# The order of the gate, up and down block products of a SwiGLU on one Trainium2 core: one by one in a mixed order, or in runs

## The chip, the cores and the metric

The kernel runs on one core of a Trainium2 chip. A core has TensorE (matmuls, results in PSUM, a memory of eight banks), VectorE, ScalarE, GpSimd (POOL in the rows) and SyncE (SP in the rows), which here issues all transfers. Each engine works through its own queue in order; engines wait for each other by semaphores. The metric is the device time of one execution in microseconds (us), the median of several.

## The reference

One encoder layer on 768 tokens (512 and 256) of width 1024, in fp32. A token mixer with three kinds of heads comes first, then

```
def swiglu(x, w_gate, w_up, w_down):
    return (jax.nn.silu(x @ w_gate) * (x @ w_up)) @ w_down

x = layer_norm(DEEPNORM_ALPHA * x + mix, ...)
x = layer_norm(DEEPNORM_ALPHA * x + swiglu(x, w_gate, w_up, w_down), ...)
```

The hidden width is 2816, that is 22 blocks of 128, worked on as 11 pairs of blocks. The change concerns the SwiGLU alone.

## The kernel before

Every fp32 operand of a matmul is split into a high and a low part (`split`, L112: a cast on ScalarE, L113, and a subtraction on VectorE or GpSimd, L114), and a product is three matmuls: high by high, high by low, low by high.

For a pair of hidden blocks, x @ w_gate, x @ w_up and the product with w_down are each a 2 by 2 block product, done with seven block products in place of eight. The seven have the names 1, 2, 6, 5, 7, 3, 4 and run in this order (`PRODUCTS`); g1 is product 1 of the gate, u4 product 4 of the up, d6 product 6 of the down part. A gate or up product is 12 matmuls of 384 columns (`gate_up`, L997, matmul L1010), a down product 9 of 512 (`down`, L1034, matmul L1043).

The sums that link the seven lie in PSUM. In the gate and up part, products 1, 6, 7 and 4 add up in one bank (bank 0 for g and u alike), 5 and 3 in another, 2 in bank 1. Between them results are taken out: after 1, 6 and 5 ScalarE copies the bank ("snap", L1021), after 2, 7 and 3 VectorE adds bank and snap (L1026), then silu (L933, gate) or the multiply with the silu (L936, up). Product 4 is read straight out of its bank, by silu or by the multiply that is called the drain below. In the down part products 1, 6, 7, 4 add up in three banks (one for each of three groups of tokens) and 2, 5, 3 in three others; after each product VectorE adds the bank into y (L1048), three adds of 512 columns.

Seven hidden blocks feed the down products: `gated` (L935) makes them after the up products, with four sums on GpSimd (L945 to L949), and splits them into seven places of `mix`, the last three in `gated_rest`.

Pair p's gate and up products run together with the down products of pair p - 1, for p = 1 to 9 (L1102 to L1111). Pair 0 stands before (`first_pair`), pair 10 and the last two down parts after. TensorE's order is the program's. The other engines' order is made by a scheduler at build time.

Weights come in blocks of 512 KB (tile `raw`, L121) into three buffers, in the order of `raws` in `_ff_items` (L1126): two of g, two of d, two of u. A block's buffer is free when its last split or sum is done. GpSimd makes the sums of blocks that products 6, 5 and 7 need (L168; L180 for the down part, after product 5's split). The split operands lie in five tiles `w` of two operands each, in the order of `items`. `op_done` (L211) frees a tile when the product with its second operand is done, and `pump` then issues up to two more splits (none after a down product).

Of the kernel before, what the change touches and what calls it, by code (L numbers as in the profile page):

```python
# [27 lines left out]
NP = NFF // 2  # L28
NP_ST = 9
PRODUCTS = (1, 2, 6, 5, 7, 3, 4)  # L30
OUT_ORDER = [6, 7, 2, 3, 4, 0, 1, 5]


# [25 lines left out]
def encoder_layer(ctx: ExitStack, tc, a, o):  # L59
# [27 lines left out]
    def catch_up(until):  # L87
        saved = clock["now"]
        while queue and queue[0][0] <= until:
            at, _, f = heapq.heappop(queue)  # L90
            clock["now"] = at
            f()
        clock["now"] = saved

    def run(main):
        for cost, f in main:
            catch_up(clock["now"])
            f()
            clock["now"] += cost
# [4 lines left out]
    items, raw_order = _ff_items()  # L104
    raw_of = {key: W_FF + i for i, key in enumerate(raw_order)}
    n_raw, n_items = W_FF + len(raw_order), W_FF + len(items)
    w_tiles = {}
    w_state = {"dma": 0, "item": 0, "free": 3}
    w_raw, w_sum, raw_done = {}, {}, set()
    w2 = []  # L110

# [81 lines left out]
    def pump(most=99):  # L193
        while w_state["item"] < n_items:
            if w_ready(w_state["item"]):
                if most == 0:
                    break
                most -= 1
                w_split()
            elif w_state["dma"] < n_raw and (w_state["dma"] < 3 or w_state["dma"] - 3 in raw_done):  # L200
                w_load()
            else:
                break
# [6 lines left out]

    def op_done(key, prod):  # L211
        n = w_tiles.pop((key, prod))[1]
        if n % 2 == 1 or n == len(items) - 1:
            w_state["free"] += 1
        if w_state.get("after") is None:
            pump()
        else:
            with tc.issue_after(w_state["after"]):
                pump(AHEAD[key[0]])
# [7 lines left out]
    def load_x(k):  # L227
        raw = rawp.tile([P, 1024], F32, tag="raw", name="raw")
        if k > 0:
            nc.sync.dma_start(out=raw[:, :T], in_=a["xT"][k])  # L230
        return raw
# [34 lines left out]
    raws = {0: load_x(0)}  # L266
# [535 lines left out]
    def x1_block(name, m, k):  # L802
        if name in ("t3", "t4"):
            return mix[k + (4 if name == "t3" else 0)][:, m, :H2]
        return xb[name][:, m, k]
# [32 lines left out]
    def wout_mm(ps, t, half, i, first, last):  # L838
        w = w_tiles[W_OUT + 4 * half + i // 2]
        sl = slice((i % 2) * 512, (i % 2 + 1) * 512)  # L840
        for m, wi in ((0, 0), (0, 1), (1, 0)):
            TE.matmul(ps, lhsT=mix[OUT_ORDER[i]][:, m, t * P:(t + 1) * P], rhs=w[:, wi, sl],  # L842
                      start=(i == first and m == 0 and wi == 0), stop=(i == last and m == 1))
# [71 lines left out]
    def bank(i):  # L915
        if i < 4:
            return pff.tile([P, 512], F32, tag=f"p{i}", name="ff")
        return ps_one({4: "sc", 5: "sc", 6: "tp", 7: "av"}[i])
# [7 lines left out]
    def gt_block(i, m):  # L926
        return mix[i][:, m, H2:]
# [7 lines left out]
    def gated(i, src, p):  # L935
        V.tensor_tensor(out=HB[i], in0=src, in1=TH[i], op=ALU.mult)  # L936
        if p >= NP_ST:
            gt_split(4 * (p - NP_ST) + i, HB[i])
            return

        if i in (0, 2):
            gt_split(i // 2, HB[i])
        have.add(i)
        if i > 0 and {0, 1, 3} <= have and i != 2:
            G.tensor_tensor(out=S1, in0=HB[1], in1=HB[3], op=ALU.add)  # L945
            G.tensor_tensor(out=HB[1], in0=HB[0], in1=HB[1], op=ALU.subtract)
            G.tensor_tensor(out=HB[0], in0=S1, in1=HB[0], op=ALU.subtract)
        if len(have) == 4:
            G.tensor_tensor(out=HB[2], in0=HB[2], in1=HB[0], op=ALU.subtract)  # L949
            gt_split(2, HB[0])  # L950
            gt_split(3, S1)
            have.clear()
# [3 lines left out]
    def gated_rest():  # L956
        gt_split(4, HB[1])
        gt_split(5, HB[2])
        gt_split(6, HB[3])
# [37 lines left out]
    def gate_up(kind, p, banks):  # L997
        st = {}

        def step(prod, k):  # L1000
            if k == 0 and prod < 3:
                st[prod] = bank(banks[prod - 1])[:, :H2]
                if prod == 2:
                    st[5] = st[2]
            elif k == 0 and prod == 5 and len(banks) > 2:
                st[5] = bank(banks[2])[:, :H2]
            b = st[{2: 2, 5: 5, 3: 5}.get(prod, 1)]
            w = w_tiles[(kind, p), prod][0]
            for wi, m in ((0, 0), (0, 1), (1, 0)):
                TE.matmul(b, lhsT=w[:, wi, k * P:(k + 1) * P], rhs=x1_block(x_name[prod], m, k),  # L1010
                          start=(prod in (1, 2, 5) and k == 0 and wi == 0 and m == 0), stop=(k == 3 and wi == 1), skip_group_check=prod in (6, 7, 4, 3))
            if k == 3:
                after(prod)
                op_done((kind, p), prod)

        def after(prod):
            use = silu if kind == "g" else lambda i, src: gated(i, src, p)
            out = TH if kind == "g" else HB
            if prod in (1, 6, 5):
                st["s", prod] = t = wk2.tile([P, H2], F32, tag="snap", name="snap", bufs=2)  # L1020
                S.copy(out=t, in_=st[5 if prod == 5 else 1])  # L1021
            elif prod == 4:
                use(2, st[1])
            else:
                i, b, other = {2: (0, 2, 1), 7: (3, 1, 5), 3: (1, 5, 6)}[prod]
                w_state["after"] = V.tensor_tensor(out=out[i], in0=st[b], in1=st["s", other], op=ALU.add).ins  # L1026
                use(i, out[i])

        return lambda prods: [(0.48, lambda prod=prod, k=k: step(prod, k)) for prod in prods for k in range(4)]
# [4 lines left out]
    def down(p):  # L1034
        st = {}

        def step(prod, t):
            if prod < 3:
                st[prod, t] = bank(2 + t if prod == 1 else 5 + t)
            b = st[1 if prod in (1, 6, 7, 4) else 2, t]  # L1040
            w = w_tiles[("d", p), prod][0]
            for m, wi in ((0, 0), (0, 1), (1, 0)):
                TE.matmul(b, lhsT=gt_block(a_slot[prod], m)[:, t * P:(t + 1) * P], rhs=w[:, wi],  # L1043
                          start=(prod in (1, 2, 5) and m == 0 and wi == 0), stop=(m == 1),
                          skip_group_check=prod in (6, 7, 4, 3))
            for dt, c in {1: ((0, lo_half),), 2: ((0, lo_half),), 6: ((0, hi_half),), 5: ((3, hi_half),),
                          7: ((3, hi_half),), 3: ((0, hi_half),), 4: ((3, lo_half),)}[prod]:
                V.tensor_tensor(out=y[t + dt][:, c], in0=b, in1=y[t + dt][:, c], op=ALU.add)  # L1048
            if t == 2:
                op_done(("d", p), prod)  # L1050

        return lambda prods: [(0.64, lambda prod=prod, t=t: step(prod, t)) for prod in prods for t in range(3)]
# [49 lines left out]
    for p in range(1, NP):  # L1102
        g = gate_up("g", p, (0, 1, 7))
        if p <= NP_ST:
            u, d = gate_up("u", p, (0, 1)), down(p - 1)
            run(g(PRODUCTS))
            run(d(PRODUCTS[:4]))
            run(u(PRODUCTS))
            run(d(PRODUCTS[4:]))
            if p < NP_ST:  # L1110
                gated_rest()  # L1111
        else:
            u = gate_up("u", p, (2, 3))
            run(g(PRODUCTS))
            run(u(PRODUCTS))
    ln2 = load_ln(1)
# [9 lines left out]
def _ff_items():  # L1126

    items = [((kind, 0), prod) for kind in "gu" for prod in (11, 12, 21, 22)]
    raws = [((kind, 0), i) for kind in "gu" for i in range(2)]
    for p in range(1, NP):  # L1130
        items += [(("g", p), prod) for prod in PRODUCTS]
        raws += [(("g", p), i) for i in range(2)]
        if p <= NP_ST:
            items += [(("d", p - 1), prod) for prod in PRODUCTS[:4]]
            raws += [(("d", p - 1), i) for i in range(2)]
        items += [(("u", p), prod) for prod in PRODUCTS]
        raws += [(("u", p), i) for i in range(2)]
        if p <= NP_ST:
            items += [(("d", p - 1), prod) for prod in PRODUCTS[4:]]
    for p in range(NP_ST, NP):  # L1140
        items += [(("d", p), prod) for prod in (11, 12, 21, 22)]
        raws += [(("d", p), i) for i in range(2)]
    return items, raws


def _layout(inputs):
# [24 lines left out]
    subs += bv[0] + bqk[0] + au + bqk[1] + bqk[2] + bv[1] + av + bqk[3]  # L1171
    wo = np.concatenate([wout[k * P:(k + 1) * P] for k in OUT_ORDER], axis=0)
    for half in range(2):
# [59 lines left out]
```

## Time and profile before

| | us |
|---|---|
| median of 3 runs | 892.03 (890.7 to 892.97) |
| the profiled execution | 893.67 |
| its span, first to last instruction | 891.8 |
| nine pairs, g1 of pair 1 to g1 of pair 10 | 428.39 |
| VectorE busy in them | 376.59 |
| GpSimd busy in them | 239.91 |

Rows of a timeline give the start, the duration (several instructions of one kind merged into one row, with their count), the engine, the line, what is written from what, and in brackets how long the engine was idle before and what ended that. The duration of one instruction overlaps the next one's by some tens of ns, so the step from start to start is the cost in a full queue.

### The profile page before, as it was taken

To read this page: it belongs to the slowest core of one execution; us is meant where nothing else is said; L and a number is where in the kernel's file an instruction comes from. 1 tells how busy PE (TensorE), PEld (TensorE's weight loads), DVE (VectorE), ACT (ScalarE), POOL (GpSimd) and SP (SyncE) were. 2 spreads that over 40 slices of the span, in tenths; PEclk is the share of its full clock that TensorE was granted. 3 is DMA by queue.
4 is the path that set the end of the run, shared out by engine and by line. 5 is a ranking of instruction groups with operands and counts; after the bars stand their busy time and mean duration, and the time that the engine had idled before them with its cause. 6 is when DMAs were issued, how large, how long until landed. Compare 5 with 4: busy or idle time off the path is not lost. (4 is left out here: it accounts for less than half of the span.)

```text
span 891.8 us, 12955 instructions
## 1 busy us (share of the span) xinstructions
PE 846.5 (95%) x4811; PEld 754.3 (85%) x4811; DVE 666.9 (75%) x1168; ACT 422.0 (47%) x922; POOL 384.7 (43%) x320
## 2 busy tenths in 40 slices
PE   7999999999999998899999999999999999899996
PEld 6889897888987887898888898898888888789985
DVE  3574447576677568769989897988979797989577
ACT  3375477676665526544434444344444344344421
POOL 0580011100121148877655655555466464653235
PEclk9999999999999999999999999999999999999999
DMA  6830202011017101112212121222121222222222
GB/s 220 247 113 24 71 26 71 24 49 46 5 54 276 54 18 50 46 48 72 72 38 81 48 82 61 72 71 72 70 71 48 71 72 71 71 70 73 72 83 107
DMA packets 22160, 66.66 MB, mean 75 GB/s; under 512 B 3664, under 2 KB 5584, under 8 KB 22096
## 3 DMA queue, kind: packets, MB, share of 16 engines
q1 hardware_dynamic: 22096, 65.82, 22.4%
q8 instruction: 38, 0.62, 0.3%
q14 instruction: 26, 0.21, 0.1%
HBM read 62.67 MB, written 3.15 MB: 74 GB/s over the span
## 5 line engine op out<-in xcount | busy, mean ns | idle before, releaser
L114 DVE TENSOR_TENSOR w<-raw,w 128x512 fp32r<-128x512 f32 (+2 forms) x179 | 185.1, 1053 | 36.3 <-ACT w L113 35.4
L113 ACT CAST w<-raw 128x512 fp32r<-128x512 f32 (+2 forms) x213 | 138.3, 676 | 119.1 <-POOL raw L168 43.8
L1010 PE MATMUL ff<-x,w 128*128 128x384 f32 x600 | 109.9, 336 | 1.7 <-DVE bv L991 1.7
L1010 PEld LDWEIGHTS ff<-x,w 128*128 128x128 f32 x600 | 105.3, 188 | 3.5 <-DVE bv L991 2.0
L1010 PE MATMUL ff<-mix,w 128*128 128x384 f32 x480 | 91.8, 339 | 14.5 <-ACT snap L1021 6.5
L1010 PEld LDWEIGHTS ff<-mix,w 128*128 128x128 f32 x480 | 83.4, 188 | 19.3 <-DVE bv L1026 9.6
L444 PE MATMUL mm<-xhi,w 128*128 128x512 f32 x320 | 79.1, 346 | 0.4 <-DVE qs L341 0.4
L168 POOL TENSOR_TENSOR ws<-raw 128x512 f32<-128x512 f32 x29 | 41.2, 1424 | 79.2 <-DMA raw<-in_w 74.9
L168 POOL TENSOR_TENSOR raw<-raw 128x512 f32<-128x512 f32 x49 | 71.2, 1454 | 6.7 <-DVE w L114 3.5
L423 PE MATMUL mm<-w,xhi 128*128 128x256 f32 x384 | 71.4, 286 | 0.0
L842 PE MATMUL mm<-w,mix 128*128 128x512 f32 x270 | 68.3, 399 | 1.5 <-ACT tt L686 0.8
L1010 PE MATMUL ff<-xt,w 128*128 128x384 f32 x360 | 65.9, 335 | 0.0
L621 POOL TENSOR_TENSOR mn<-mn,neghalf 128x1 f32<-128x1 f32 x24 | 13.8, 574 | 116.6 <-DVE mn L620 112.8
L1010 PEld LDWEIGHTS ff<-xt,w 128*128 128x128 f32 x360 | 63.0, 188 | 0.0
L1043 PE MATMUL ff<-w,mix 128*128 128x512 f32 x216 | 58.2, 400 | 4.9 <-DVE y L1048 4.9
L842 PEld LDWEIGHTS mm<-w,mix 128*128 128x128 f32 x270 | 49.2, 188 | 12.6 <-ACT tt L686 1.3
L423 PEld LDWEIGHTS mm<-w,xhi 128*128 128x128 f32 x384 | 58.1, 189 | 1.4 <-issue 0.9
L444 PEld LDWEIGHTS mm<-xhi,w 128*128 128x128 f32 x320 | 49.1, 189 | 6.8 <-issue 0.8
L114 DVE TENSOR_TENSOR mix<-bv,mix 128x384 fp32r<-128x384 f32 x62 | 52.9, 856 | 2.1 <-ACT mix L113 2.0
L114 POOL TENSOR_TENSOR w<-raw,w 128x512 fp32r<-128x512 f32 x34 | 49.6, 1475 | 10.5 <-ACT w L113 10.2
L1043 PE MATMUL sc<-w,mix 128*128 128x512 f32 x189 | 50.4, 398 | 3.4 <-DVE y L1048 3.4
L423 PE MATMUL mm<-w,xlo 128*128 128x256 f32 x192 | 53.4, 278 | 0.0
(234 smaller groups left out, 1772.8 us busy)
## 6 DMA issues: line engine op xcount, KB each, us to landing
raw<-in_w SPq DMA_DIRECT2D x95, 512.0 KB, 3.3
y<-in_x SPq DMA_DIRECT2D x6, 512.0 KB, 9.2
out_y<-y SPq DMA_DIRECT2D x12, 256.0 KB, 2.0
raw<-in_xT SPq DMA_DIRECT2D x7, 384.0 KB, 5.2
ln<-in_lng SPq DMA_DIRECT2D x2, 512.0 KB, 7.2
ln<-in_lnb SPq DMA_DIRECT2D x2, 512.0 KB, 7.6
rpb<-in_rpbs SPq DMA_DIRECT2D x32, 30.6 KB, 3.4
rpb<-in_rpbp SPq DMA_DIRECT2D x16, 59.6 KB, 3.1
```

What stands on the lines that cost most here:

```text
L113: S.copy(out=hi, in_=src)
L114: eng.tensor_tensor(out=lo, in0=src, in1=hi.bitcast(F32), op=ALU.subtract)
L168: G.tensor_tensor(out=out, in0=in0, in1=in1, op=f)
L423: TE.matmul(ps, lhsT=x[:, k, t * P:(t + 1) * P], rhs=w[:, wi, sl], start=(k == 0 and x is xhi and wi == 0), stop=(k == KT - 1 and x is xlo))
L444: TE.matmul(p, lhsT=w[:, wi, sl], rhs=x[:, k, c0:c1], start=(k == 0 and wi == 0 and x is x_hi), stop=(k == KT - 1 and wi == 1))
L621: G.tensor_tensor(out=mn[:, 7:8], in0=mn[:, 7:8], in1=neghalf[:, 0:1], op=ALU.pow)
L842: TE.matmul(ps, lhsT=mix[OUT_ORDER[i]][:, m, t * P:(t + 1) * P], rhs=w[:, wi, sl], start=(i == first and m == 0 and wi == 0), stop=(i == l ...
L1010: TE.matmul(b, lhsT=w[:, wi, k * P:(k + 1) * P], rhs=x1_block(x_name[prod], m, k), start=(prod in (1, 2, 5) and k == 0 and wi == 0 and m = ...
L1043: TE.matmul(b, lhsT=gt_block(a_slot[prod], m)[:, t * P:(t + 1) * P], rhs=w[:, wi], start=(prod in (1, 2, 5) and m == 0 and wi == 0), stop= ...
```

## The change

The order of products on TensorE within a pair p is now a table, `MIXED`, with single products: the gate products first, d1 before g4, then down and up products in turn, and u3 and u4 last. The order in which operands are split is a second table, `SPLIT_ORDER`, close to it. Two operands that share a tile can now be used out of order, so `op_done` counts finished operands and frees tiles from the oldest on ("tail"). The order of the blocks of weights is the same as before.

```
+SPLIT_ORDER = ("g1", "g2", "g6", "g5", "g7", "g3", "d1", "g4", "d2", "d6", "u1", "d5", "u2", "d7", "d3", "u6", "d4",
+               "u5", "u7", "u3", "u4")
+MIXED = ("g1", "g2", "g6", "g5", "g7", "g3", "d1", "g4", "d2", "u1", "d6", "u2", "d5", "u6", "d7", "u5", "d3",
+         "u7", "d4", "u3", "u4")
...
-        if n % 2 == 1 or n == len(items) - 1:
+        ops_done.add(n)
+
+        while w_state["tail"] in ops_done and (w_state["tail"] + 1 in ops_done or w_state["tail"] == len(items) - 1):
+            w_state["tail"] += 2
             w_state["free"] += 1
...
-            u, d = gate_up("u", p, (0, 1)), down(p - 1)
-            run(g(PRODUCTS))
-            run(d(PRODUCTS[:4]))
-            run(u(PRODUCTS))
-            run(d(PRODUCTS[4:]))
+            part = {"g": g, "u": gate_up("u", p, (0, 1)), "d": down(p - 1)}
+            for m in MIXED:
+                run(part[m[0]]((int(m[1]),)))
...
-        items += [(("g", p), prod) for prod in PRODUCTS]
-        raws += [(("g", p), i) for i in range(2)]
-        if p <= NP_ST:
-            items += [(("d", p - 1), prod) for prod in PRODUCTS[:4]]
-            raws += [(("d", p - 1), i) for i in range(2)]
-        items += [(("u", p), prod) for prod in PRODUCTS]
-        raws += [(("u", p), i) for i in range(2)]
-        if p <= NP_ST:
-            items += [(("d", p - 1), prod) for prod in PRODUCTS[4:]]
+        kinds = "gdu" if p <= NP_ST else "gu"
+        items += [((m[0], p - (m[0] == "d")), int(m[1])) for m in
+                  (SPLIT_ORDER if p <= NP_ST else [kind + str(prod) for kind in kinds for prod in PRODUCTS])]
+        raws += [((kind, p - (kind == "d")), i) for kind in kinds for i in range(2)]
```

Lines after the diff's first part lie 7 to 10 lower in the new kernel: L114 is L121 there, L936 L946, L1010 L1020, L1026 L1036, L1043 L1053, L1048 L1058.

TensorE at the end of pair 1 and the start of pair 2, before: u3 and u4 (`x` and `mix`), the three last down products, then g1 and g2.

```order
L1010 MATMUL ff<-x_3554,w 128x384 x12
L1010 MATMUL ff<-mix,w 128x384 x12
L1043 MATMUL ff<-w,mix 128x512 x6
L1043 MATMUL sc<-w,mix 128x512 x6
L1043 MATMUL tp<-w,mix 128x512 x3
L1043 MATMUL av<-w,mix 128x512 x3
L1043 MATMUL ff<-w,mix 128x512 x6
L1043 MATMUL sc<-w,mix 128x512 x3
L1010 MATMUL ff<-x_3552,w 128x384 x12
```

And in the changed kernel, from u7 on: the last down product lies before u3, and g1 follows u4.

```order
L1020 MATMUL ff<-mix,w 128x384 x12
L1053 MATMUL ff<-w,mix 128x512 x6
L1053 MATMUL sc<-w,mix 128x512 x3
L1020 MATMUL ff<-x_3554,w 128x384 x12
L1020 MATMUL ff<-mix,w 128x384 x12
L1020 MATMUL ff<-x_3552,w 128x384 x12
L1020 MATMUL ff<-x_3553,w 128x384 x12
```

The three down products (6 + 6 + 3 + 3 + 6 + 3 matmuls) that stood between u4 and g1 have moved up between the up products.

VectorE of the changed kernel at the end of pair 2, from the last add into y to the drain of u4 and a little on. `w` is a weight split, `mix` a split of a hidden block, `bv` the hidden blocks, `ffs` the silu's results.

```order
L1058 TENSOR_TENSOR y_3127<-sc,y_3127 128x512
L121 TENSOR_TENSOR mix<-bv,mix 128x384
L1036 TENSOR_TENSOR bv<-ff,snap 128x384
L121 TENSOR_TENSOR w<-raw,w 128x512 x4
L946 TENSOR_TENSOR bv<-bv,ffs 128x384
L946 TENSOR_TENSOR bv<-ff,ffs 128x384
L121 TENSOR_TENSOR mix<-bv,mix 128x384
L121 TENSOR_TENSOR mix<-gs_3924,mix 128x384
```

Four weight splits stand between the add of u3 (L1036) and the drain (the second L946); at the end of odd pairs they are three. Before, the adds into y of the last three down products followed the drain.

ScalarE of the changed kernel at the start of pair 3, the end of the casts of hidden blocks and the first snap of the gate products.

```order
L120 CAST mix<-bv 128x384 x2
L120 CAST w<-raw 128x512
L120 CAST mix<-gs_3924 128x384
L120 CAST w<-raw 128x512
L120 CAST mix<-bv 128x384
L1031 COPY snap<-ff 128x384
L120 CAST mix<-bv 128x384
```

The two casts of `raw` are those of d2 and d6; at the start of even pairs the cast of d6 and the third `mix<-bv` come after the snap. Later in the same pair the silu of g4, which reads the bank, stands behind the cast of u6:

```order
L943 ACTIVATE ffs<-ffs 128x384
L120 CAST w<-raw 128x512
L943 ACTIVATE ffs<-ffs 128x384
L120 CAST w<-raw 128x512
L943 ACTIVATE ffs<-ff 128x384
```

The first cast here is d3's, the second u6's. Before, four down products lay between g4 and u1 on TensorE; now it is d2 alone.

## Rows read from the trace of the kernel before

**Rows 1.** The page: its span, and the busy time of each engine.

```profile
span 891.8 us, 12955 instructions
...
PE 846.5 (95%) x4811; PEld 754.3 (85%) x4811; DVE 666.9 (75%) x1168; ACT 422.0 (47%) x922; POOL 384.7 (43%) x320
```

**Rows 2.** Busy time by window, one window for each of the pairs 1 to 9 (here pair 3 and the sum). Columns: window and length, busy time and instructions of PE, PEld, DVE, ACT and POOL, granted clock of TensorE, share and rate of DMA.

```profile
491.02:537.34 46.32, 44.88 (x233) 40.67 (x231) 39.98 (x57) 20.41 (x40) 27.03 (x20) 1.00 0.24 76
...
sum 428.39, PE 403.87 PEld 367.39 DVE 376.59 ACT 179.69 POOL 239.91; mean PE 44.87 PEld 40.82 DVE 41.84 ACT 19.97 POOL 26.66
```

**Rows 3.** Timeline of TensorE: the starts of the runs g, d, u, d in the first and in the last of the nine pairs (and of the pair after each), then the first two rows of pair 10's up run and the row after them.

```profile
393.38 2.25 PE L1010 MATMUL ff<-x,w 128*128 128x384 f32 x12
...
412.77 1.55 PE L1043 MATMUL ff<-w,mix 128*128 128x512 f32 x6
...
420.97 4.39 PE L1010 MATMUL ff<-x,w 128*128 128x384 f32 x24
...
436.29 1.55 PE L1043 MATMUL ff<-w,mix 128*128 128x512 f32 x6
...
443.24 4.37 PE L1010 MATMUL ff<-x,w 128*128 128x384 f32 x24
...
776.10 4.33 PE L1010 MATMUL ff<-x,w 128*128 128x384 f32 x24
...
790.79 1.54 PE L1043 MATMUL ff<-w,mix 128*128 128x512 f32 x6
...
800.53 4.35 PE L1010 MATMUL ff<-x,w 128*128 128x384 f32 x24
...
815.61 1.55 PE L1043 MATMUL ff<-w,mix 128*128 128x512 f32 x6
...
821.77 4.35 PE L1010 MATMUL ff<-x,w 128*128 128x384 f32 x24
...
840.68 4.32 PE L1010 MATMUL ff<-xt,w 128*128 128x384 f32 x24
844.84 2.24 PE L1010 MATMUL ff<-mix,w 128*128 128x384 f32 x12
```

**Rows 4.** Table of waits of TensorE, whole span: total, times, longest.

```profile
PE ff L1010 <- ACT snap L1021: 6.5, 5, 1.5
...
PE ff L1043 <- DVE y L1048: 4.9, 10, 0.7
```

**Rows 5.** Timeline of TensorE and VectorE in the first down run of pair 3.

```profile
509.48 0.68 DVE L1048 TENSOR_TENSOR y<-ff,y 128x512 f32<-128x512 f32 x1
...
510.21 0.96 PE L1043 MATMUL ff<-w,mix 128*128 128x512 f32 x3 [0.34 <-DVE y L1048]
...
511.16 0.68 DVE L1048 TENSOR_TENSOR y<-ff,y 128x512 f32<-128x512 f32 x1
...
511.76 1.27 DVE L1048 TENSOR_TENSOR y<-sc,y 128x512 f32<-128x512 f32 x2
...
511.90 0.97 PE L1043 MATMUL ff<-w,mix 128*128 128x512 f32 x3 [0.72 <-DVE y L1048]
```

**Rows 6.** Timeline around the drain of u4, at the end of pair 2 and of pair 3: the first down matmuls after u4, the add of u3 (L1026), the multiply and the drain (L936 from `ff`).

```profile
484.69 1.55 PE L1043 MATMUL ff<-w,mix 128*128 128x512 f32 x6
...
486.03 0.54 DVE L936 TENSOR_TENSOR bv<-ff,ffs 128x384 f32<-128x384 f32 x1
...
530.37 0.55 DVE L1026 TENSOR_TENSOR bv<-ff,snap 128x384 f32<-128x384 f32 x1
...
530.42 1.55 PE L1043 MATMUL ff<-w,mix 128*128 128x512 f32 x6
...
530.95 0.56 DVE L936 TENSOR_TENSOR bv<-bv,ffs 128x384 f32<-128x384 f32 x1
531.42 0.55 DVE L936 TENSOR_TENSOR bv<-ff,ffs 128x384 f32<-128x384 f32 x1
```

**Rows 7.** Timeline of VectorE, weight splits: two with GpSimd at work beside them, and one with GpSimd idle.

```profile
483.99 2.11 DVE L114 TENSOR_TENSOR w<-raw,w 128x512 fp32r<-128x512 f32 x2
...
491.66 0.68 DVE L114 TENSOR_TENSOR w<-raw,w 128x512 fp32r<-128x512 f32 x1
```

**Rows 8.** Timeline of GpSimd and SP in pair 3: the last sum of the down part, the load into the buffer that it frees, and the sums over the two blocks of u.

```profile
499.71 1.68 POOL L180 TENSOR_TENSOR ws<-raw 128x512 f32<-128x512 f32 x1 [1.23 <-DVE w L114]
...
501.42 0.33 SPq L121 DMA_DIRECT2D raw<-in_w  x1
...
504.63 1.29 POOL L168 TENSOR_TENSOR ws<-raw 128x512 f32<-128x512 f32 x1 [3.24 <-DMA raw<-in_w]
506.00 1.30 POOL L168 TENSOR_TENSOR raw<-raw 128x512 f32<-128x512 f32 x1
507.38 1.62 POOL L168 TENSOR_TENSOR raw<-ws,raw 128x512 f32<-128x512 f32 x1
```

**Rows 9.** Timeline of ScalarE, GpSimd and TensorE in the gate run of pair 4: a silu, the snap behind it, L180 and the matmul that waited for the snap.

```profile
546.34 0.52 ACT L933 ACTIVATE ffs<-ffs 128x384 f32<-128x384 f32 x1 [1.84 <-DVE ffs L1026]
546.77 0.46 ACT L1021 COPY snap<-ff 128x384 f32<-128x384 f32 x1
...
546.98 1.68 POOL L180 TENSOR_TENSOR ws<-raw 128x512 f32<-128x512 f32 x1 [1.56 <-DVE w L114]
...
547.28 2.36 PE L1010 MATMUL ff<-mix,w 128*128 128x384 f32 x12 [1.46 <-ACT snap L1021]
```

More of the change, by code (lines that the diff above doesn't have):

```diff
@@ L107, in encoder_layer @@
     w_tiles = {}
-    w_state = {"dma": 0, "item": 0, "free": 3}
+    w_state = {"dma": 0, "item": 0, "free": 3, "tail": 0}
+    ops_done = set()
     w_raw, w_sum, raw_done = {}, {}, set()
```

## The prediction

> **What bounds the kernel now.** I read the page first: TensorE is busy 95% of the span and VectorE 75% [rows 1]. The change touches one stage, the nine pairs p = 1 to 9 of the SwiGLU, so next I read busy time by window, one window for each pair. The nine take 428.39 us together; TensorE's clock is 1.00 in all of them, and VectorE is busy 376.6 us of them, 88% [rows 2]. So TensorE leads in this stage and VectorE has little to spare.
>
> Then TensorE's timeline gives the work without waits. In the undisturbed run of pair 10 two up products take 844.84 − 840.68 = 4.16 us, so 2.08 each; the last run of three down products takes 821.77 − 815.61 = 6.16, so 2.05 each [rows 3]. A pair is 14 × 2.08 + 7 × 2.05 = 43.47 us, nine are 391.2. The stage holds 428.4 − 391.2 = 37.2 us of waits, 4.1 a pair. Taking the starts of the runs in all nine pairs in the same way (first and last pair shown in rows 3), the waits lie thus: gate runs 12.1 (4.8 of it in pair 1: 412.77 − 393.38 − 14.56), first four down products 11.0, up runs 10.1, last three down products 3.9.
>
> The table of waits names two of the causes, the adds into y and the copy of a partial sum ("snap") [rows 4]; the timeline shows how they act. In a down run TensorE adds the next product onto the bank that VectorE has just to add into y: it waits for L1048 at 510.21 and 511.90, while VectorE works off its queue at 0.60 us per add (1.27 for two) [rows 5]. In a gate run a product waits for ScalarE's snap, which stands behind a silu that waits for VectorE [rows 9]. Both are queues that come in lumps.
>
> **The change part by part.** No arithmetic is added or removed; matmuls, adds, splits and loads keep number and size. What moves is who stands between two users of a bank.
>
> *Gone: waits inside the down and up products.* d1 and d6 use the same banks. Before, d2 alone (2.05 us) stood between; now g4, d2 and u1 do, 2.08 + 2.05 + 2.08 = 6.2 us, and every later repeat in d or u has 4.1 us (u7 to u4) or more. Three adds are 1.8 us of VectorE, so these waits should vanish: 11.0 + 10.1 + 3.9 = 25.0 us. What is late next is below. The gate run keeps its order but for d1 before g4; I take its own 7.3 us of pairs 2 to 9 out too and put the new gate waits in from the order.
>
> *New, first: u4 stands directly before the next g1, on the same bank 0.* Before, three down products (6.15 us) lay between. The reader of u4's bank is the multiply that drains it (L936), and g1 waits for it. Queued behind that multiply's place are g1, then g2 and everything after on TensorE. What did this drain need before? It ended at 531.97, 1.55 us after u4's matmuls gave way to d7 at 530.42, and in the pair before at 486.57, 1.88 after 484.69 [rows 6]. That is the low bound: 9 × 1.6 = 14 us. By the new order VectorE has, from the end of u7 (6.2 us before u4's end): add of u7, two splits, multiply, three y adds, one hidden split, add of u3, then four (into odd pairs and into pair 10) or three weight splits (into even pairs), multiply, drain. At 0.47 us for a 384-wide step (530.95 to 531.42) and 0.60 for a 512-wide one [rows 5, 6] that is 6 × 0.47 + 9 × 0.60 = 8.2 us or 7.6. I allow 0.15 us for start and end, and in the odd case another 0.5 us, an estimate, for the hidden split, whose cast stands behind four others on ScalarE: g1 starts 2.8 us late into odd pairs, 1.7 into even ones. 5 × 2.8 + 4 × 1.7 = 20.8 us. High bound: a split takes 0.68 us with POOL quiet but 1.06 where POOL works beside it [rows 7]; with the latter the splits add 4 × 0.45 or 3 × 0.45, 14 us more in all.
>
> The Trainium skill, SBUF — State Buffer, section Who interferes with whom, says that a VectorE instruction with two SBUF inputs and a GpSimd instruction that reads SBUF block each other for a whole instruction. The trace agrees in size (0.68 against 1.06); by that rule this sum would be 20.8 only while POOL idles before the drain, and 35 if it does not.
>
> *New, second: the gate run of odd pairs.* ScalarE's queue there has g1's snap behind the cast of d6's operand and of a hidden block, and both behind POOL; POOL's step waits for a block of w_down whose buffer is freed only by one of the splits ahead of the drain (0.7 us after u4). A load lands 3.2 us after its issue (501.42 to 504.63) and a POOL sum takes 1.4 [rows 8]; so 0.7 + 3.2 + 1.4 + 1.4 (a POOL step on the hidden blocks, taken as long as a sum) + two casts and the snap (some 1.3) = 8.0 us, while TensorE is at g6 at 2.8 + 4.16 = 7.0: 1.0 us. The same queue, with two more POOL steps, makes g7 wait for g6's snap about 1.0 more. 4 × 2.0 = 8 us. In even pairs the snap stands ahead of these: 0. Bounds: 0, if the loads are earlier, and 2 × 1.5 us (the longest snap wait of before, rows 4) in all eight pairs, 24.
>
> *New, third: u1 before the silu of g4.* Both use bank 0; before, four down products (8.2 us) lay between, now d2 alone. On ScalarE the silu stands behind the cast of u6's operand, which needs three POOL sums after a load that waits for L180. In pair 3 L180 ends at 501.39, 10.4 us after g1; the third sum at 509.00, 7.6 later [rows 2, 8]. In pair 4 L180 ends 11.3 after g1 [rows 2, 9]; then the third sum is at 18.9, cast and silu make it 19.9, and u1 wants the bank at 7 × 2.08 + 2 × 2.05 = 18.7: 1.2 us. Odd pairs have lost 2 us in the gate run, which covers it; in pair 1 I take 1.2 as well. 5 × 1.2 = 6 us; bounds 0 and 9 × 2.
>
> *The same:* pair 1's gate run waits for the first pair's work, 4.8 us, and its order is unchanged. Operand supply: the splits still run up to five operand tiles ahead; three buffers for raw blocks now serve d and u in turns, and their delays are in the second and third term; SP's queue keeps its order of blocks (two of g, two of d, two of u); beyond these I cost the supply at nothing, since TensorE waited for no weight split in this stage. After pair 10's g1 nothing changes.
>
> Sum: 20.8 + 8 + 6 + 4.8 = 39.6 us of waits against 37.2: +2.4 on the profiled execution's 893.67, 896.1. That execution lies 1.6 above the median of the three runs, 892.03, so 894.4 for the median; I say 894.5. The change frees 25 us and spends them again at three new narrow places.
>
> **The rivals.**
> *The queues keep up (faster).* Only the drain before g1 stays; loads and POOL come early enough, so snaps and silu never hold TensorE. For it: the y adds no longer pile up ahead of the gate run, and before, the snap waits came behind such a pile [rows 9]. Against it: ScalarE's order has the POOL-bound casts ahead of the snap. Waits 20.8 + 4.8 = 25.6, so 11.6 us less: 880.
>
> *VectorE is stuck on a late operand before the drain (slower).* The two splits that follow u7's add are of g6 and g5, and g6 needs POOL's third sum over two new gate blocks. The block's load waits for POOL's split of u3. If the third sum ends later than u7's end, all that stands behind it on VectorE, the drain last, moves out one for one, and POOL then works beside the four splits. I place that sum about 3 us early; from 3 us of delay on (one load at twice its time) this decides. Priced with the slow splits, 1.4 to 1.8 us a pair, 14 us: 908.
>
> *The change doesn't spread the work.* VectorE is at 88%; were it the bound, the order of TensorE would not matter and the time stay within a microsecond of 892. Against it: VectorE's busy time contains the slow splits, and in these pairs TensorE's waits sit at a few places, not everywhere. I count this into the forecast, which lies next to it.
>
> **How the numbers follow.** Forecast (the waits change places) 0.50, with its own range 888 to 901; queues keep up 0.32; stuck on a late operand 0.18. A measurement of this kernel can tell 0.3%, 2.7 us, from no change. The forecast spreads some 5 us either way about 894.5: of its 0.50, 0.09 fall under 889.4, 0.19 between, 0.22 over 894.7. The faster rival gives 0.30 faster and 0.02 same, the slower 0.175 slower. Together faster 0.39, same 0.21, slower 0.40. The range goes from 878 to 908, to the price of both rivals; wider only if two bounds meet.
>
> **What would show it.** Right: TensorE's waits for y are gone from the table; L1020's g1 waits for L946 in every pair, 1.5 to 3 us; odd gate runs wait for snap, even ones hardly; u1 waits for L943 in even pairs; pairs of 46 and 48 us in turn. Wrong: pairs under 46 us throughout, or waits for y left over; or VectorE idle for more than 2 us on a cast ahead of the drain, which is the slower rival. The forecast falls if g1 waits under 1 us, since that is half of the new cost.

## The result and the profile after

The changed kernel takes 900.1 us (median of 4 runs, 898.86 to 901.11), the kernel before, on the same chip, 892.5 (890.7 to 893.89): ratio 1.0094, 95% interval 1.0078 to 1.0109. It is slower. The forecast was 894.5; the range 878 to 908 holds the result. The profiled execution takes 900.12.

The page after, with [rows 1] for before. The added lines move the line numbers by 7 to 10: L1010 is now L1020 (gate and up matmul), L1043 is L1053 (down matmul), L936 is L946 (multiply and drain), L933 is L943 (silu), L1021 is L1031 (snap).

```profile
span 898.2 us, 12951 instructions
...
PE 850.6 (95%) x4811; PEld 761.8 (85%) x4811; DVE 649.4 (72%) x1168; ACT 421.5 (47%) x922; POOL 381.1 (42%) x320
```

Busy time by window, one window for each pair (here pair 3 and the sum), columns as in [rows 2]:

```profile
491.30:539.05 47.75, 46.15 (x232) 42.66 (x232) 39.31 (x56) 19.84 (x39) 26.67 (x20) 0.96 0.20 67
...
sum 434.67, PE 406.78 PEld 373.52 DVE 361.67 ACT 178.56 POOL 235.07; mean PE 45.20 PEld 41.50 DVE 40.19 ACT 19.84 POOL 26.12
```

All of the loss is in the nine pairs: 434.67 − 428.39 = 6.3 us, while the profiled executions differ by 900.12 − 893.67 = 6.45. VectorE's busy time fell by 15 us and the stage still grew. The granted clock is 0.96 in pair 3 (also in 5 and 7), where before it was 1.00 in every pair. TensorE's table of waits, against [rows 4]:

```profile
PE ff L1020 <- DVE bv L946: 16.9, 9, 2.2
PE ff L1020 <- ACT ffs L943: 7.4, 5, 1.6
...
PE ff L1020 <- ACT snap L1031: 2.6, 4, 1.1
```

No wait for y is left. In its place stand two waits that were not there: for the drain of u4, nine times, and for the silu of g4, five times. Timeline around the first, between pairs 2 and 3 (TensorE's u4 and g1; VectorE's work from u3's add on; GpSimd's first step after a long rest). VectorE's four splits and the multiply stand ahead of the drain at 490.70, with GpSimd idle: 0.60 us a split. It answers to [rows 6].

```profile
486.87 2.24 PE L1020 MATMUL ff<-mix,w 128*128 128x384 f32 x12
...
487.36 0.55 DVE L1036 TENSOR_TENSOR bv<-ff,snap 128x384 f32<-128x384 f32 x1
487.82 2.49 DVE L121 TENSOR_TENSOR w<-raw,w 128x512 fp32r<-128x512 f32 x4
490.23 0.55 DVE L946 TENSOR_TENSOR bv<-bv,ffs 128x384 f32<-128x384 f32 x1
490.70 0.55 DVE L946 TENSOR_TENSOR bv<-ff,ffs 128x384 f32<-128x384 f32 x1
...
490.86 1.01 POOL L955 TENSOR_TENSOR gs<-bv 128x384 f32<-128x384 f32 x1 [9.88 <-DVE bv L946]
...
491.30 6.03 PE L1020 MATMUL ff<-x,w 128*128 128x384 f32 x24 [2.19 <-DVE bv L946]
```

The second, in pair 2: on ScalarE the silu stands behind a cast that waits for GpSimd's sum, and u1 behind the silu.

```profile
462.70 0.62 ACT L120 CAST w<-raw 128x512 fp32r<-128x512 f32 x1 [3.86 <-POOL raw L175]
463.22 0.48 ACT L943 ACTIVATE ffs<-ff 128x384 f32<-128x384 f32 x1
...
463.76 2.35 PE L1020 MATMUL ff<-x,w 128*128 128x384 f32 x12 [1.39 <-ACT ffs L943]
```

The 6.03 us of g1 and g2 at 491.30 are the surprise: two products take 4.5 elsewhere. Windows of 1 us from there on (the last three columns: granted clock, share and rate of DMA):

```profile
491.00:492.00 1.00, 0.70 (x4) 0.70 (x5) 0.42 (x2) 0.51 (x1) 0.87 (x1) 1.00 0.89 299
492.00:493.00 1.00, 1.00 (x6) 1.00 (x5) 0.38 (x1) 0.47 (x1) 0.44 (x1) 0.77 0.81 262
493.00:494.00 1.00, 1.00 (x5) 1.00 (x5) 0.41 (x1) 0.69 (x3) 1.00 (x2) 0.50 0.56 221
...
496.00:497.00 1.00, 1.00 (x8) 1.00 (x7) 1.00 (x1) 0.04 (x1) 1.00 (x2) 1.00 0.00 0
```

TensorE waits 2.19 us, starts at full clock, and about 1 us later the granted clock is at its lower level (0.50 of full, 1.2 GHz in place of 2.4) for some 3 us. The same happens at the start of pairs 5 and 7, after waits of 2.14, but not at that of pair 9, after the same wait of 2.19. Pair 9 waits for a snap later instead:

```profile
779.80 4.46 PE L1020 MATMUL ff<-x,w 128*128 128x384 f32 x24 [2.19 <-DVE bv L946]
...
790.20 2.35 PE L1020 MATMUL ff<-mix,w 128*128 128x384 f32 x12 [1.05 <-ACT snap L1031]
```

Below this is called a slow stretch. It takes 6.03 − 4.46 = 1.6 us more of TensorE each time.

### The profile page after: what moved, and what is told of

Its sections match the earlier page's. It is cut to its first block, busy times and chain, and to the rows that moved or that the text cites. A ratio compares the mean times of both kernels' runs of the same rounds, so it can differ in the third digit from the quotient of the medians.

```text
span 898.2 us, 12951 instructions
## 1 busy us (share of the span) xinstructions
PE 850.6 (95%) x4811; PEld 761.8 (85%) x4811; DVE 649.4 (72%) x1168; ACT 421.5 (47%) x922; POOL 381.1 (42%) x320
## 5 line engine op out<-in xcount | busy, mean ns | idle before, releaser
L121 DVE TENSOR_TENSOR w<-raw,w 128x512 fp32r<-128x512 f32 (+2 forms) x179 | 178.5, 1015 | 57.4 <-ACT w L120 57.2
L1020 PE MATMUL ff<-x,w 128*128 128x384 f32 x600 | 117.9, 349 | 25.0 <-DVE bv L946 16.9
L1020 PEld LDWEIGHTS ff<-x,w 128*128 128x128 f32 x600 | 109.2, 195 | 32.8 <-DVE bv L946 19.8
L1020 PE MATMUL ff<-mix,w 128*128 128x384 f32 x480 | 91.1, 338 | 2.4 <-ACT snap L1031 2.2
L1020 PEld LDWEIGHTS ff<-mix,w 128*128 128x128 f32 x480 | 84.3, 188 | 5.9 <-ACT snap L1031 4.0
L121 POOL TENSOR_TENSOR w<-raw,w 128x512 fp32r<-128x512 f32 x34 | 49.6, 1469 | 63.1 <-ACT w L120 63.1
L175 POOL TENSOR_TENSOR raw<-raw 128x512 f32<-128x512 f32 x49 | 73.1, 1491 | 3.4 <-DVE w L121 0.7
L120 ACT CAST mix<-bv 128x384 fp32r<-128x384 f32 x62 | 31.6, 511 | 87.5 <-DVE bv L946 62.9
L1020 PE MATMUL ff<-xt,w 128*128 128x384 f32 x360 | 67.7, 336 | 0.4 <-ACT snap L1031 0.4
L1020 PEld LDWEIGHTS ff<-xt,w 128*128 128x128 f32 x360 | 63.5, 188 | 2.3 <-ACT snap L1031 0.7
L121 DVE TENSOR_TENSOR mix<-bv,mix 128x384 fp32r<-128x384 f32 x62 | 53.9, 871 | 12.2 <-ACT mix L120 11.8
L1053 PE MATMUL ff<-w,mix 128*128 128x512 f32 x216 | 55.7, 393 | 0.0
L1053 PE MATMUL sc<-w,mix 128*128 128x512 f32 x189 | 53.8, 393 | 0.0
```

Of the source, the lines that this page charges most:

```text
L120: S.copy(out=hi, in_=src)
L121: eng.tensor_tensor(out=lo, in0=src, in1=hi.bitcast(F32), op=ALU.subtract)
L175: G.tensor_tensor(out=out, in0=in0, in1=in1, op=f)
```

## The experiments

Ratios are to the kernel before, timed beside each on the same chip. "Stage" is the nine pairs of the profiled execution. Where a gap is given, it is the step between the starts of two products less 2.08 for a gate or up product and 2.05 for a down product, as in the prediction.

**Other banks for the up run.**

```
-            part = {"g": g, "u": gate_up("u", p, (0, 1)), "d": down(p - 1)}
+            part = {"g": g, "u": gate_up("u", p, (1, 0)), "d": down(p - 1)}
```

> The up run's two banks change places (up's 1, 6, 7, 4 on bank 1, its 2, 5, 3 on bank 0), so that the next g1 no longer shares a bank with u4, nor u1 with g4. Theory (the stage lost its time at the two bank waits, 16.9 us before g1 and 7.4 us before u1, and at the three stretches of clock 0.50 behind the first of them, about 3 x 1.6 = 4.8 us): both waits and the three stretches are gone, stage of the nine pairs 434.7 - 29.1 = 406 us (402 to 412), run about 871 us. Rival A (VectorE or the operands bound the stage, 361.7 us busy in it): the waits come back at other products, stage over 425, run over 890. Rival B (the clock falls for another reason than the wait before g1): waits gone, the 0.50 stretches at the starts of pairs 3, 5 and 7 stay, stage about 411.

871.24 us, ratio 0.9734 (0.9713 to 0.9755). The stage is 404.4, neither bank wait is left, the clock is 1.00 in every pair. The largest waits of the stage:

```profile
PE ff L1020 <- DVE ffs L1036: 3.0, 5, 0.8
...
PE ff L1020 <- ACT snap L1031: 1.2, 2, 1.0
```

The sum of the two waits and the slow stretches was right to within 2 us. Timeline at the start of pair 3 (TensorE's g1 and g2, VectorE's drain of u4, the first step of ScalarE after g1):

```profile
486.29 4.70 PE L1020 MATMUL ff<-x,w 128*128 128x384 f32 x24
...
488.04 0.55 DVE L946 TENSOR_TENSOR bv<-ff,ffs 128x384 f32<-128x384 f32 x1
...
488.66 0.48 ACT L1031 COPY snap<-ff 128x384 f32<-128x384 f32 x1 [4.81 <-PE ff L1020]
```

g1 starts 1.75 us before the drain does, so it is the other bank that lets it go. But the scheduler also ordered ScalarE anew: in odd pairs the snap of g1 now stands ahead of the casts that it stood behind in the changed kernel. So this one edit changed two things, and that the 4.8 us of the slow stretches came right with the rest is in part luck: further down (d6 ahead of u1) a pair without the stretch loses the same time to the snap as long as the old order stands. Rival A falls: VectorE is busy 368.7 us in a stage of 404 and doesn't bound it.

**d4 behind u4.**

```
-         "u7", "d4", "u3", "u4")
+         "u7", "u3", "u4", "d4")
```

> d4 is computed behind u4 instead of ahead of u3, so that 2 us of work stand between u4 and the next g1; u1 still follows g4 closely. Theory: the 16.9 us of waits before g1 and the clock's three stretches (4.8) are gone, the 7.4 us before u1 stay: stage 434.7 - 21.7 = 413 us, run about 878. Rival A (VectorE bounds): stage over 425, waits at other products. Rival B (clock independent of the wait): stage about 418, 0.50 stretches stay.

880.98, ratio 0.9852 (0.9831 to 0.9874); stage 416.6. The waits before g1 are gone. But slow stretches appear at other places, in pairs 2, 4 and 8, behind a new wait for the snap of g5. TensorE's g3 and ScalarE's queue in pair 2:

```profile
455.09 1.14 ACT L120 CAST w<-raw 128x512 fp32r<-128x512 f32 x2 [2.76 <-DMA raw<-in_w]
456.13 0.47 ACT L1031 COPY snap<-av 128x384 f32<-128x384 f32 x1
...
456.65 3.74 PE L1020 MATMUL av<-x,w 128*128 128x384 f32 x12 [2.40 <-ACT snap L1031]
```

The snap waits behind two casts whose block has not landed. TensorE's lead at g1 is partly given back at the next thing that comes late, a load.

**d6 ahead of u1.**

```
-MIXED = (..., "g4", "d2", "u1", "d6", "u2", ...
+MIXED = (..., "g4", "d2", "d6", "u1", "u2", ...
```

> d6 changes places with u1, so that two down products instead of one stand between g4 and u1; the end of the pair is as in the changed kernel. Theory: only the 7.4 us before u1 go, the waits before g1 (16.9 us) and the clock's three stretches stay: stage 427 us, run about 893. Rival A: the time moves to other waits, stage 433 to 436, run about 900.

892.5, ratio 0.9981 (0.9967 to 0.9994); stage 426.2. The waits for silu are gone, the drain's stand at 17.2 us, as the theory said. Its windows hold a finding, pairs 3, 5 and 7:

```profile
488.80:536.52 47.72, 45.93 (x231) 42.61 (x232) 38.29 (x56) 19.83 (x39) 26.48 (x20) 0.96 0.22 67
...
583.19:630.83 47.64, 44.64 (x231) 41.01 (x232) 38.77 (x56) 19.92 (x39) 26.32 (x20) 1.00 0.21 66
...
677.63:725.27 47.64, 45.88 (x231) 42.60 (x231) 38.59 (x56) 20.03 (x39) 26.35 (x20) 0.96 0.20 67
```

Pair 5 has no slow stretch and takes as long as 3 and 7. Its gate run has gaps of 0.47 and 1.25 us, for the snaps of g1 and g6, where the others have 0.4 or less at g6's snap. The slow stretch lies ahead of a wait and uses it up.

**Matmuls that nobody reads, between u4 and g1.**

```
+            fill = bank(7)[:, :H2]
+            for i in range(12):
+                TE.matmul(fill, lhsT=xb["11"][:, 0, 0, :P], rhs=xb["11"][:, 0, i % 4], start=True, stop=True)
```

> Twelve matmuls of 384 columns (2.08 us) that write bank 7 and are never read stand between u4 and the next g1, so that TensorE is busy while it would wait for the drain. Theory (the idle time before g1 brings the clock down in pairs 3, 5 and 7): no 0.50 stretches, -4.8 us; the even gaps of 1.7 us grow to 2.1 (4 to 5 of them, +1.8): stage about 431.7 us, run about 897. Rival B (the clock falls for another reason): 0.50 stretches stay, stage about 436.5, run about 902.

900.51, ratio 1.0066 (1.0048 to 1.0084); stage 435.7. The clock is 1.00 in all nine pairs, so the slow stretches do hang on the idle time. But the 4.8 us did not come: the theory's price was wrong. The table of waits (lines are one higher here):

```profile
PE ff L1021 <- ACT ffs L944: 10.9, 9, 1.5
```

What the gate runs gained (gaps of 7.9 us in the stage, 12.7 in the changed kernel), u1's wait took: it now waits for silu in all nine pairs. In the changed kernel the odd pairs' lost time had covered that.

**The other banks alone, in the kernel before.**

```
-            u, d = gate_up("u", p, (0, 1)), down(p - 1)
+            u, d = gate_up("u", p, (1, 0)), down(p - 1)
```

> The kernel before (runs of seven, four, seven and three) with the up run's two banks exchanged alone. Theory (the bank order costs only where u4 is followed at once by g1 and g4 almost at once by u1, as in the mixed order; in runs, down products stand between): no change, ratio 0.998 to 1.002, run about 892.5, the waits for the y additions stay. Rival (the exchange of the banks is worth some 29 us whatever the order is, and mixing is worth nothing): about 865.

891.44, ratio 0.9996 (0.9985 to 1.0008). Nothing, as the theory said. The banks cost time only in the mixed order, and the gain of the first experiment is the mixing's.

**The drain ahead of the splits.** `op_done` issues no split after u3, and up to four after u4, behind its multiply:

```
+                if key[0] == "u" and 0 < key[1] <= NP_ST and prod in (3, 4):
+                    pump(0 if prod == 3 else 4)
+                else:
+                    pump(AHEAD[key[0]])
...
+        if i == 2 and p > 0:
+            w_state["after"] = mult.ins
```

> The changed kernel, with VectorE's four weight splits that stand between u3's addition and the read of u4's bank put behind that read, and no other order changed on purpose. Theory (g1 waits for u4's read because it is queued behind splits): the read follows u4's last matmul at once, each gap before g1 falls from 1.7 to 2.35 us to 0.7 to 0.9, no 0.50 stretch at the start of an odd pair; the waits for snap in odd pairs (1.7 each, as pair 5 of the order with d6 ahead of u1 shows them without the stretch) and before u1 stay: stage 434.7 - 10 = 424 to 426 us, run about 890. Rival (the four splits are needed that early): new waits of the g products or d1 for a split, stage 432 or more, run 898 or more.

902.54, ratio 1.0118 (1.0101 to 1.0135); stage 439.7. No gain, where some 10 us were said; beside the changed kernel's 1.0094 (1.0078 to 1.0109) it is slower by little more than the noise. The drain waits fell as said (0.8 us at each g1), but the others grew (lines 3 to 5 higher here):

```profile
PE ff L1025 <- ACT ffs L946: 15.6, 9, 3.2
PE ff L1025 <- ACT snap L1036: 8.0, 7, 1.7
PE ff L1025 <- DVE bv L949: 5.9, 9, 0.7
```

VectorE and the load at the end of pair 5, first in the changed kernel, then with the drain ahead:

```profile
632.13 1.88 DVE L121 TENSOR_TENSOR w<-raw,w 128x512 fp32r<-128x512 f32 x3
...
632.87 19.91 SPq L128 DMA_DIRECT2D raw<-in_w  x4
```

```profile
633.84 1.56 POOL L961 TENSOR_TENSOR bv<-bv 128x384 f32<-128x384 f32 x1
...
633.85 3.53 DVE L121 TENSOR_TENSOR w<-raw,w 128x512 fp32r<-128x512 f32 x3
...
634.60 18.75 SPq L128 DMA_DIRECT2D raw<-in_w  x4
```

The splits now start 1.7 us later and run beside GpSimd, 3.53 us for three in place of 1.88; the next load (the first of the four merged in the row), whose buffer such a split frees, is issued 1.7 us later, and behind it come GpSimd's sums, the cast and the silu. How much of the loss the load makes is not shown: the scheduler also put three of GpSimd's steps on the hidden blocks ahead of its sum of weights, which starts 3.0 us later (639.15 in place of 636.19). And behind the waits for silu in pairs 2, 6 and 8 (2.2 to 3.2 us) the granted clock falls: u1 and d6 take 5.9 us more in the nine pairs than in the changed kernel, while the slow stretches at g1 are gone. The rival named the wrong consumer (a split that a matmul waits for); that the splits are needed that early fits the rows. That VectorE and GpSimd hold each other up is what the Trainium skill says (SBUF — State Buffer, Who interferes with whom), and here the trace agrees: 3.53 us against 1.88 for three splits.

**The operands in the order of the products.**

```
-                  (SPLIT_ORDER if p <= NP_ST else [kind + str(prod) for kind in kinds for prod in PRODUCTS])]
+                  (MIXED if p <= NP_ST else [kind + str(prod) for kind in kinds for prod in PRODUCTS])]
```

> The changed kernel, with the operands split and loaded in exactly the order of the products instead of the second table's order. Theory (operands come early enough in either order, the order of the products alone makes the time): 900, within 898 to 903, with the waits before g1 (16.9 us) and u1 (7.4 us). Rival (the second table is what keeps the operands in time): over 905, with waits for splits before d or u products.

909.7, ratio 1.0199 (1.0176 to 1.0223); stage 440.2. The rival is nearer, though no product waits for a split: the drain's waits grew.

```profile
PE ff L1020 <- DVE bv L946: 28.1, 9, 4.8
```

VectorE ahead of the drain at the end of pair 9, GpSimd beside it, and g1:

```profile
830.00 2.35 DVE L121 TENSOR_TENSOR w<-raw,w 128x512 fp32r<-128x512 f32 x2
...
830.01 1.79 POOL L175 TENSOR_TENSOR ws<-raw 128x512 f32<-128x512 f32 x1 [8.47 <-DMA raw<-in_w]
...
832.28 1.61 DVE L946 TENSOR_TENSOR bv<-bv,ffs 128x384 f32<-128x384 f32 x1
...
834.41 6.87 PE L1020 MATMUL ff<-x,w 128*128 128x384 f32 x24 [4.18 <-DVE bv L946]
```

GpSimd's sums fall beside the splits; a split takes over 1.1 us and the multiply 1.61 in place of 0.55. This is half of the prediction's slower rival, the slow splits beside GpSimd; the other half, a VectorE that stands on a late operand, doesn't show. The second table of the change keeps the sums away from the drain. Slow stretches add to the loss: the granted clock is at its lower level behind the drain's wait at the start of pairs 2, 4, 5, 6, 8, 9 and 10, of which the last makes g1 and g2 take 6.87 us.

**d6 ahead of u1, and the unread matmuls.** Both edits from above.

> d6 ahead of u1 (no wait before u1 is left) and the twelve unread matmuls between u4 and g1 together. The order with d6 ahead of u1 alone gave 892.5 us, stage 426.2, with the 0.50 stretch in pairs 3, 7, 9 and 10 and without it in pair 5, and its pairs 3, 5 and 7 all took 47.6 to 47.7: where TensorE was slow no wait for snap followed, where it was not 1.7 us of it did. Theory (the slow stretch costs next to nothing here, since it lies ahead of a wait that it uses up): no slow stretch, 1.2 to 1.8 us of waits for snap in the odd pairs, stage 425 to 428, run about 893. Rival (each slow stretch costs its 1.6 us): stage about 420, run about 887.

886.83, ratio 0.9916 (0.9902 to 0.9929); stage 420.9. The rival's numbers. But the scheduler had also changed ScalarE's order, here and in the kernel with the unread matmuls alone: the casts of the hidden blocks, which wait for GpSimd, stood ahead of the copies of g1 and g6, and now stand behind. Pair 5 with d6 ahead of u1 alone, and then with both:

```profile
586.98 0.51 ACT L120 CAST mix<-bv 128x384 fp32r<-128x384 f32 x1 [0.67 <-POOL bv L956]
587.40 0.47 ACT L1031 COPY snap<-ff 128x384 f32<-128x384 f32 x1
```

```profile
585.89 0.47 ACT L1032 COPY snap<-ff 128x384 f32<-128x384 f32 x1
586.66 0.52 ACT L121 CAST mix<-bv 128x384 fp32r<-128x384 f32 x1 [0.29 <-POOL bv L957]
```

g1 starts at 583.19 in the first and at 582.83 in the second, so the copy comes 3.06 us after it in place of 4.21. So the run didn't tell the clock from the order, which the next one does.

**The order of these casts alone.** Every engine's order as in the last kernel but without the unread matmuls. The main part of the edit, for odd pairs (`silu` and `snap` are kept where those instructions are issued, not shown):

```
+                if m == "g2" and p > 1 and p % 2:
+                    with tc.issue_after(w_state["silu"]):
+                        gt_split(2, HB[0])
...
+            with tc.issue_after(w_state["snap"]) if p % 2 else ExitStack():
+                gt_split(4, HB[1])
...
+            with tc.issue_after(w_state["snap"]) if p % 2 else ExitStack():
+                gt_split(5, HB[2])
```

> d6 ahead of u1, without the unread matmuls, and with the order on ScalarE and VectorE that the kernel with d6 ahead of u1 and unread matmuls got: in odd pairs the casts of the gated halves that wait for GpSimd stand behind the copies of g1 and g6 and not ahead of them. That kernel took 886.8 us (stage 420.9), d6 ahead of u1 alone 892.5 (stage 426.2); they differ in this order and in the unread matmuls, which hold the clock up. If the order alone made the difference: the odd pairs lose no time to snap, stage 420 to 421, run about 886. If the clock alone made it: slow stretches at odd pairs as before, stage about 426, run about 892. If each only uncovers the other (a slow stretch costs its 1.6 us once no wait for snap follows): slow stretches in 3 to 5 pairs, no wait for snap, stage 424 to 427, run about 891, and an odd pair without a slow stretch, if there is one, takes about 46 us against 47.6.

889.28, ratio 0.9933 (0.991 to 0.9956), between the first case and the third; stage 422.7. Pairs 3, 5 and 7:

```profile
488.82:535.05 46.23, 44.35 (x231) 41.02 (x231) 39.68 (x56) 19.55 (x39) 26.94 (x20) 1.00 0.22 69
...
581.82:628.13 46.31, 44.38 (x232) 41.08 (x232) 39.56 (x56) 19.54 (x39) 26.63 (x20) 1.00 0.22 69
...
674.87:722.12 47.25, 45.63 (x231) 42.66 (x231) 39.77 (x56) 20.13 (x39) 27.00 (x20) 0.96 0.21 67
```

With the copies first, an odd pair without the slow stretch takes 46.2 to 46.3 in place of 47.6: the order is worth 1.4 us. With the slow stretch (pair 7) it takes 1.0 more. So, as far as these few pairs show it, the stretch costs nothing where a wait for snap follows, and 1.0 of its 1.6 us where none does.

**Both covers by order alone.** d4 behind u4 and d6 ahead of u1, banks as in the changed kernel.

> d4 behind u4 and d6 ahead of u1 together, the banks as in the changed kernel: cover by order alone. Theory (cover by a product is as good as another bank at u1 and g1, but the waits of even pairs for snap, 2.7 us in pairs 2, 4 and 8 of the order with d4 last, with the slow stretches behind them, come from the loads and stay): only the 3.5 us before u1 go, run about 877. Rival (any cover is worth what the exchange of the banks is worth): run about 871.

877.32, ratio 0.9811 (0.9798 to 0.9825); stage 409.2. The time is the theory's, 0.4% less than with d4 last alone:

```profile
PE av L1020 <- ACT snap L1031: 7.4, 3, 2.5
```

The three waits for g5's snap stay, as said. That no slow stretch stands behind them was not said; it takes the stage 4 us lower than the theory has it, but the profiled execution (875.21) is also the fastest of the five. By the ratios, cover by order is worth 0.8% less than the other bank.

**Other banks, and d2 ahead of g4.**

```
-MIXED = (..., "d1", "g4", "d2", "u1", "d6", ...
+MIXED = (..., "d1", "d2", "g4", "u1", "d6", ...
...
-            part = {"g": g, "u": gate_up("u", p, (0, 1)), "d": down(p - 1)}
+            part = {"g": g, "u": gate_up("u", p, (1, 0)), "d": down(p - 1)}
```

> The version with exchanged banks, and d2 ahead of g4 in the order (g3, d1, d2, g4, u1), so that g4, which adds onto the bank that g7's addition reads, comes 2 us later. Theory: the waits of 0.65 to 1.0 us before g4 in most pairs go and nothing takes their place: stage 404.4 - 4.5 = 400 us, run about 867. Rival: u2 now follows g4 by one product and waits for silu, or d2 waits for bank 7 that g3's addition reads: stage 404 to 408, run 871 to 875.

868.95, ratio 0.9736 (0.972 to 0.9752), no better than other banks alone (0.9734). The stage is 402.6, 1.7 less, where 4.5 were said. The waits before g4 are gone, but d2 now waits for bank 7, as the rival said: in pairs 2 to 9 its last three matmuls start late and its step is 0.3 to 1.2 us over 2.05. In pair 3:

```profile
500.18 0.96 PE L1053 MATMUL av<-w,mix 128*128 128x512 f32 x3 [0.39 <-DVE ffs L1036]
```

Either version beats both kernels.

## Why the prediction came out as it did

It held in sign and in range, the sign by little: the forecast of +2.5 us lay within the 2.7 us that it calls no change, slower had a chance of 0.40 against 0.39 for faster, and the +7.6 measured are three times the forecast. The profiled execution was put at 896.1 and took 900.12. Of the 4.0 us, 3.9 are the sum of gaps in the stage: 39.6 forecast, 434.67 − 391.2 = 43.5 measured. The total is a small difference of large terms, and their misses partly cancel, which is luck. By its terms (sums of gaps over the pairs):

| term | forecast | measured |
|---|---|---|
| waits for y, in d | gone | gone |
| u4's drain before g1 | 20.8 | 18.5 |
| gate run of odd pairs 3 to 9 | 8 | 8.7 |
| silu of g4 before u1, with the products after g3 | 6 | 9.1 |
| pair 1's gate run | 4.8 | 2.2 |
| gate run of even pairs | 0 | 1.9 |
| u1 to u4 | 0 | 3.1 |

The prediction closes its sum with 25 us freed and spent again; its own terms have 32.3 freed, the gate run's 7.3 among them, and 34.8 spent.

*Gone.* Right, and the banks experiment shows that it is worth more than the loss: with the two collisions away, mixing saves 2.7%.

*The drain before g1.* Right in place, mechanism and size. From VectorE's order the wait was put at 2.8 us into odd pairs and 1.7 into even; the gaps are 2.3 and 1.7. The hidden split's extra 0.5 us did not come, and GpSimd idled ahead of the drain, so the low price of a split held.

*The snap in odd pairs.* Right in sum. The cause is there as said in pair 9 (gaps of 0.6 and 1.2 us), and in the order with d6 ahead of u1, where 1.4 us a pair go with the casts behind the copies. But in pairs 3, 5 and 7 of the changed kernel the slow stretch, which nothing in the trace of before announced, stands in most of its place. That this miss cost almost nothing, because the stretch uses up the wait, is luck.

*The silu before u1.* In the right pairs (1, 2, 4, 6, 8), but this term was mis-sized: 1.6 to 1.8 us each, not 1.2. In pair 2 the silu ends 463.70 − 442.93 = 20.8 us after g1, where 19.9 was worked out. That odd pairs are covered by what they lose in the gate run was right too: the unread matmuls took that loss away, and u1 waited there as well.

*Pair 1's gate run* was carried over unchanged at 4.8. But 1.5 of it stood before g4, and d1 now lies there; another 1.0 fell away before g2, for a reason that was not looked for.

*The d and u products cost nothing.* This step failed by 3.1 us. No single wait stands there. 1.0 of it is u1's own step, 0.07 to 0.15 us over 2.08 in each pair; the ten other products take 0.02 more than 2.08 or 2.05 on average. The same products in the kernel before, where they did not wait, took 0.01 to 0.02 more as well, some 1 us over the nine pairs, which the prediction counted among the waits that go. TensorE goes from one kind of product to another 14 times in a pair where it did so 4 times before; what that costs is not shown.

*Pairs of 46 and 48 in turn* did not come: 47.6 to 47.8 (pairs 3, 5 and 7) and 48.4 to 48.6 (even), since the drain and the odd gate runs nearly level them; pair 9, which ends with the longer drain wait, took 48.3. *The last step,* from profiled execution to median, took off 1.6; here the two are equal.

*The rivals.* "Queues keep up": the loads and GpSimd do hold snap and silu. "VectorE bounds": the banks experiment refutes it. The slower rival didn't come about by itself; with the operands in the order of the products, its slow splits do (909.7).

## What to carry to other kernels

When products are mixed so that one bank gets more cover, list the pairs of users of every bank anew, the step over the end of the loop too: here the two pairs that lost their cover took back more than all others gained, and exchanging two bank numbers, with the order of the queues that the scheduler made for it, turned a loss of 0.9% into a gain of 2.7%. Ahead of moving a drain forward in its queue, look at what the work behind it frees: the splits that were put behind released the next load, and the kernel gained nothing. An experiment that adds or moves instructions can reorder other queues, so compare the order on every engine before reading a difference as the effect of the edit.

## What the hardware showed that was not expected

The granted clock can fall to its lower level after a wait of TensorE of only 2.2 us, for about 3 us. In this stage it did so only at a wait: in the changed kernel in three of the five gate runs that follow a gap of 2.3 us (with d6 ahead of u1 likewise in some), in the kernel with d4 last at three snap waits, with the drain ahead at three waits for silu, and with the operands in the order of the products at six drain waits; in each of the last two kernels one stretch lasted twice as long. The two mixed kernels with other banks, whose largest wait in the stage is 1.0 by the table of waits, and those with unread matmuls show none. But a wait doesn't decide it: pair 9 of the changed kernel and the three waits of up to 2.5 us with both covers by order kept the full clock, and so did the kernel before at its longest wait, 2.8 us in pair 8:

```profile
767.55 2.35 PE L1010 MATMUL ff<-mix,w 128*128 128x384 f32 x12 [2.79 <-DVE bv L1026]
```

What decides was not found. The price depends on what comes next: 1.6 us of TensorE's time at half the clock, but between 0 and 1.0 us of the kernel's in the pairs that could be compared.
